# Down projections with the weight sums behind the casts, the last weight buffer taken last, and three attention output tiles ended one after another

## The chip, the cores and the metric

The kernel runs on one core of one Trainium2 chip. The metric is the device time of one execution in microseconds (us). Work is spread over five engines with a queue of their own each, and every queue is worked off in order: TensorE (PE, matrix products), VectorE (DVE), ScalarE (ACT), GpSimd (POOL) and SyncE (SP, which here issues nearly all transfers from HBM). An instruction that must wait holds up all that stands behind it in its queue.

## The reference

A decoder trunk of two layers on one sequence of 512 positions and 1024 channels, in float32. Layer 0 mixes tokens with a gated DeltaNet; then keys and values are projected once; layer 1 uses causal sliding-window attention on them. Each layer ends with a gated feed-forward part (FFN):

```
def conv_gated_mlp(hn, w_up, conv_w, conv_b, w_down):
    u = causal_dwconv(hn @ w_up, conv_w, conv_b)
    gate, val = jnp.split(u, 2, axis=-1)
    return (jax.nn.silu(gate) * val) @ w_down
```

with w_up from 1024 to 2 x 2816 channels and w_down from 2816 back to 1024. The change concerns `@ w_down` of both layers and the end of the attention's output projection `@ w_o`.

## The kernel before

Every large product is made of three matmuls in a reduced format: a weight block in a stage buffer is split by `cast` into a high part `whi` (a copy on ACT, line 132) and a low part `wlo` (a subtraction on DVE, line 133); activations are split likewise, and PE adds high x high, high x low, low x high. `cast_to` (lines 155 and 156) does the same into a part of a weight buffer that `weights()` has taken. There are three buffers each for `whi` and `wlo`, two stages named `stage`, and a third one, `st` in the profile, which every third load of a down projection uses. A cast must wait until PE has read the buffer that it reuses; a load must wait until the last cast has read its stage. SP issues the loads in the order of the program.

The FFN is done in two groups of columns of the inner dimension per layer (12 and 10 tiles of 128), so there are four down projections. Each works through four column pairs of the output (256 columns, `m2` 0 to 3), and for each of them `seven_products` does a Strassen-Winograd scheme: instead of eight products of half-size blocks seven, with sums of weight blocks made on DVE. The weights of a column pair come in two loads, block u = 0 and u = 1 (three and three, or three and two, pairs of k tiles), and a stage holds four kinds of 128-column pieces A11, A12, A21, A22. Per block the code

- adds A22 to A21 (line 1063), casts the first half of the stage, and makes two products ("B11" and "B21", banks `d` and `g` of PSUM),
- makes A11 = A21 - A11 and A12 = A12 - A11 (lines 1071, 1072), casts the second half, and makes two products ("T1" and "T4", banks `s` and `p`, or `d` again for odd column pairs),
- makes A22 = A22 - A11 (line 1080).

After the products of block 1 the results are added to h (`add`, line 1057). I call these two rounds the second phase when block 1 is meant. In the third phase both blocks' first halves are cast again, for the products "T2" and "B22", and A22 is cast with `cast_to` into `w4`, for the product "T3" (bank `g` or `p`). The generators of column pairs 0 and 1 are advanced in turns (0, 1, 0, 0, 1, 1), pairs 2 and 3 run alone; the last pair of the last group is done plainly. The order within each queue is set by a scheduler from the code's order and from estimated times, so the lines of several generators mix.

The stage of block 0 becomes free with its piece of `w4` (line 156), and SP then loads a block of a later column pair, or of the next up projection (line 122), into it.

In the attention, the output projection of the first three of eight tiles is drawn into the stream of the scores; the last k tile of these three is added at the end (line 1380) when the last heads' values are there, and line 1382 adds the tiles to h. `ah` and `al` are the high and the low part of the attention's values. The other five tiles are cast and multiplied afterwards (`out_tile`, `mm3`).

Of the kernel before, what the change touches and what calls it, by code (L numbers as in the profile page):

```python
# [12 lines left out]
ALU = mybir.AluOpType  # L13
# [4 lines left out]
P = 128  # L18
# [23 lines left out]
def kernel(  # L42
# [27 lines left out]
    V, S, G, PE, SP = nc.vector, nc.scalar, nc.gpsimd, nc.tensor, nc.sync  # L70
# [9 lines left out]
    def nm(s):  # L80
        cnt[0] += 1
        return f"{s}_{cnt[0]}"
# [30 lines left out]
    def bank(tag):  # L113
        return psum.tile([P, T], F32, tag=tag, bufs=BANKS[tag], name=nm(tag))

    def const(shape, dt=F32, s="c"):
        return cp.tile(list(shape), dt, name=nm(s))


    def load_stage(w, r0, kt, c0):  # L120
        st = wpool.tile([P, 8, 256], F32, tag="stage", bufs=2, name=nm("stage"))
        SP.dma_start(st[:, :kt, :], tiles_of(w, r0, kt, c0))
        return st
# [4 lines left out]
    def cast(st, kt, half, m=P):  # L128
        hi = wpool.tile([P, 8, P], F32R, tag="whi", bufs=3, name=nm("whi"))
        lo = wpool.tile([P, 8, P], F32R, tag="wlo", bufs=3, name=nm("wlo"))  # L130
        src = st[:, :kt, half * P : half * P + m]
        S.copy(hi[:, :kt, :m], src)  # L132
        V.tensor_tensor(lo[:, :kt, :m], src, hi[:, :kt, :m].bitcast(F32), op=ALU.subtract)  # L133
        return hi, lo
# [14 lines left out]
    def weights():  # L149
        return [wpool.tile([P, 8, P], F32R, tag=t, bufs=3, name=nm(t)) for t in ("whi", "wlo")]  # L150

    def cast_to(w, at, src):
        n = src.shape[1]
        hi, lo = [t[:, at : at + n, :] for t in w]
        S.copy(hi, src)
        V.tensor_tensor(lo, src, hi.bitcast(F32), op=ALU.subtract)
# [50 lines left out]
    first = wpool.tile([P, 8, 256], F32, tag="stage", bufs=2, name=nm("stage"))  # L207
# [55 lines left out]
    for k in range(KD):  # L263
        ps = bank("g") if k % 2 else bank("s")
# [136 lines left out]
    nk = const([P, 8, NC], s="nk")  # L401
# [365 lines left out]
    for i, line in enumerate(ORDER):  # L767
        for word in line.split():
            a, n = word[0], [int(d) for d in word[1:]]
# [41 lines left out]
    def wide(role):  # L811
        return pair(nxt("wide", YROLE), F32R)
# [6 lines left out]
    for h2 in range(HV // 2):  # L819
        a, b = wide("G"), wide("L")  # L820
# [11 lines left out]
    hT = [h4[:, m, :] for m in range(4)] + [h22[m // 2][:, m % 2, :] for m in range(4)]  # L832
# [14 lines left out]
    for m2 in range(KD // 2):  # L847
        sts = [load_stage(a_w_out[0], 1024 * u, 8, 256 * m2) for u in range(2)]
        for j in range(2):
            m = 2 * m2 + j  # L850
            ps = bank("d")
            for u in range(2):
                w = cast(sts[u], 8, j)
# [185 lines left out]
    def seven_products(sts, srcs, parts, sevens, hp, odd):  # L1039
        h11, h12, h21, h22 = [hp[:, i, HALF[u]] for i in range(2) for u in range(2)]  # L1040
        n = len(sevens)

        def blocks(u):
            e, o = slice(0, 2 * len(parts[u]), 2), slice(1, 2 * len(parts[u]), 2)
            return sts[u][:, e, 0:P], sts[u][:, o, 0:P], sts[u][:, e, P : 2 * P], sts[u][:, o, P : 2 * P]

        def product(ps, w, at, form, u, first=True, step=2):
            for i, k in enumerate(parts[u]):
                hi, lo = sevens[k][form]
                wk = at + step * i  # L1050
                kw = dict(skip_group_check=not first)
                PE.matmul(ps, w[0][:, wk, :], hi, start=first and k == 0, stop=False, **kw)  # L1052
                PE.matmul(ps, w[0][:, wk, :], lo, start=False, stop=False, **kw)  # L1053
                PE.matmul(ps, w[1][:, wk, :], hi, start=False, stop=k == n - 1, **kw)  # L1054

        def add(dst, ps):
            V.tensor_tensor(dst, dst, ps, op=ALU.add)

        a, b, d, c = [bank(t)[:, 0:256] for t in ("d", "g", "s", "d" if odd else "p")]
        for u in range(2):  # L1060
            A11, A12, A21, A22 = blocks(u)
            nk, end = len(parts[u]), u == 1
            V.tensor_tensor(A21, A21, A22, op=ALU.add)
            w = cast(sts[u], 2 * nk, 0)
            product(a, w, 0, "B11", u)
            if end:
                add(h11, a)
            product(b, w, 1, "B21", u)
            if end:
                add(h11, b)  # L1070
            V.tensor_tensor(A11, A21, A11, op=ALU.subtract)
            V.tensor_tensor(A12, A12, A11, op=ALU.subtract)
            w = cast(sts[u], 2 * nk, 1)
            product(d, w, 0, "T1", u)
            if end:
                add(h22, d)
            product(c, w, 1, "T4", u)
            if end:
                add(h21, c)
            V.tensor_tensor(A22, A22, A11, op=ALU.subtract)  # L1080
            yield
        e = bank("p" if odd else "g")[:, 0:256]
        w4 = weights()
        for u in range(2):
            w = cast(sts[u], 2 * len(parts[u]), 0)
            product(a, w, 0, "T2", u, first=False)
            product(d, w, 1, "B22", u, first=False)
            cast_to(w4, 4 * u, blocks(u)[3])

        add(hp.rearrange("p u (v t) -> p (u v) t", v=2)[:, 1:4, :], a.unsqueeze(1).to_broadcast([P, 3, 256]))  # L1090
        add(h12, d)
        for u in range(2):
            product(e, w4, 4 * u, "T3", u, step=1)
        add(hp[:, 1, :].rearrange("p (u t) -> p u t", u=2), e.unsqueeze(1).to_broadcast([P, 2, 256]))
        yield
# [68 lines left out]
    def attention(h):  # L1164
# [6 lines left out]
        for kv in range(2):  # L1171
# [3 lines left out]
            for i in range(2):  # L1175
                ps = bank("d")
# [115 lines left out]
        def values(u):  # L1292
            p, n0 = u // 2, 2 * (u % 2)
            g = p // 2
            if n0 == 0:
                heads[p] = bank("p")
            po = heads[p]
            for i in range(2):
                pT, kb0, W = heads[u, i]
                nt = W // P  # L1300
                for kb in range(nt):
                    for j in range(2):
                        PE.matmul(  # L1303
                            po[half[j], (n0 + i) * P : (n0 + i + 1) * P],
                            Vp[:, kb0 + kb, 64 * g : 64 * g + 64],
                            pT[:, (j * nt + kb) * P : (j * nt + kb + 1) * P],
                            start=kb == 0,
                            stop=kb == nt - 1,
                        )
            if n0 == 0:  # L1310
                return
            if p % 2 == 0:
                at[:] = [wide("G"), wide("L")]
            a, b = at[0][:, p % 2, :], at[1][:, p % 2, :]
            split(po[:], a, b)
            ah.append(a)
            al.append(b)


        def out_tile(m, sts={}):  # L1320
            if m % 2 == 0:
                sts[m // 2] = load_stage(b_w_o[0], 0, 8, 128 * m)
            return bank("d"), cast(sts[m // 2], 8, m % 2)
# [10 lines left out]
        def late_outputs(opened, ks):  # L1334
            for k in ks:
                for ps, w in opened:
                    yield from one_by_one(ps[:], w, k, ah[k], al[k], False, False)

        at, opened = [], []

        def dense():
            for p in range(2, 8):
                yield from query(p)
            yield from early_outputs(opened)

        def take(stream, n):
            for _ in range(n):
                next(stream, None)
# [8 lines left out]
        with tc.manual_schedule(engines={mybir.EngineType.PE}):  # L1357
            stream = dense()
            for u in range(16):
                scores(u)  # L1360
                if u > 1:
                    values(u - 2)
                if u == 1:
                    take(stream, 8)
                if u > 0:
                    turn_back(u - 1)
                take(stream, 4 if u == 1 else 12 if u < 12 else 11)
            for _ in stream:
                pass
            rest = late_outputs(opened, range(begun, KD - 1))  # L1370
            take(rest, 9)
            turn_back(15)
            values(14)
            take(rest, 5)
            values(15)
            for _ in rest:
                pass
            for i in range(3):
                for m, (ps, w) in enumerate(opened):
                    PE.matmul(ps[:], w[i % 2][:, KD - 1, :], (ah, ah, al)[i][-1], start=False, stop=i == 2)  # L1380
                    if i == 2:
                        V.tensor_tensor(hT[m], hT[m], ps[:], op=ALU.add)
        for m in range(3, KD):
            ps, w = out_tile(m)
            mm3(ps[:], w, KD, ah, al)
# [59 lines left out]
```

## Time and profile before

| what | value |
|---|---|
| runs before | 1421.04, 1417.68, 1419.02 us; median 1419.02 |
| profiled execution | 1418.66 us, its span 1416.8 us |
| granted PE clock over the span | 0.998 |
| busy PE, DVE, ACT, POOL | 98%, 78%, 53%, 1% |
| the four down projections with their neighbourhood | 657 to 722, 828 to 886, 1178 to 1242, 1347 to 1392 us |
| end of the three drawn tiles of the attention | 1015 to 1021 us |

A timeline row gives the start in us, the duration, the engine, the line, the operation, out<-in by the names in the program, the shape, and how many like rows it stands for; in brackets the idle time of the engine ahead of it and what released it. A row of waits gives who waited for whom, and then the total, how often, and the longest. The rows on transfers give the KB of each and the median time from issue to landing.

### The profile page before, as it was taken

How to read it: one execution, taken by the hardware profiler on the slowest of the kernel's cores; microseconds unless marked ns; L12 is line 12 of the kernel's file. 1: busy time of each engine (PE TensorE's matmuls, PEld its weight loads, DVE VectorE, ACT ScalarE, POOL GpSimd, SP SyncE). 2: the span in 40 equal slices, each digit the busy share in tenths (PEclk: the TensorE clock that was granted, in tenths of full speed). 3: DMA queues.
4: the chain of work that ended last, by engine and by line, in shares of the span. 5: the costliest groups of instructions: out<-in, count | busy, mean ns of one | idle time of the engine just before them, and what ended most of it. 6: DMA issues, size and time to landing. Idle time of an engine off the chain costs nothing.

```text
span 1416.8 us, 21740 instructions
## 1 busy us (share of the span) xinstructions
PE 1384.8 (98%) x8362; PEld 1166.5 (82%) x8362; DVE 1109.1 (78%) x2072; ACT 748.0 (53%) x1470; POOL 15.7 (1%) x37
## 2 busy tenths in 40 slices
PE   7999999999999999999999999999999999999997
PEld 5787888878877888888988889778788888988897
DVE  4996886968856447879878889788658888878996
ACT  7764576656647325444335446567544444444543
POOL 1000000000100000000000000000000000000000
PEclk9999999999999999999999999999999999999999
DMA  5333254172465323221443223322132221432222
GB/s 160 90 104 115 80 174 124 60 230 84 143 221 157 119 86 115 90 90 46 134 149 119 75 73 108 109 76 76 60 112 86 93 90 59 137 107 86 95 75 75
DMA packets 162299, 151.80 MB, mean 107 GB/s; under 512 B 24148, under 2 KB 150677, under 8 KB 162197
## 3 DMA queue, kind: packets, MB, share of 16 engines
q1 hardware_dynamic: 159938, 150.22, 33.0%
q8 instruction: 66, 1.08, 0.3%
q10 hardware_dynamic: 2259, 0.20, 0.1%
q14 instruction: 36, 0.29, 0.1%
HBM read 133.60 MB, written 15.75 MB: 105 GB/s over the span
## 4 chain that ended last, share of the span: by engine, by line
PE 85%; DVE 7%; DMA 4%; ACT 2%; issue 1%; SPq 0%; DVEq 0%; ACTq 0%
PE d L162 20%; PE d L164 20%; PE d L163 20%; PE g L198 2%; DVE wlo L133 2%; PE d L1207 1%; PE d L1211 1%; PE d L1209 1%; PE d L1054 1%; PE d L1052 1%; PE d L1053 1%; PE s L1054 1%; PE p L1303 1%; PE s L659 1%; PE s L1052 1%
## 5 line engine op out<-in xcount | busy, mean ns | idle before, releaser
L162 PE MATMUL d<-xh,whi 128*128 128x512 f32 x1128 | 444.2, 394 | 0.2
L163 PE MATMUL d<-xl,whi 128*128 128x512 f32 x1128 | 444.0, 394 | 0.0
L164 PE MATMUL d<-xh,wlo 128*128 128x512 f32 x1128 | 442.1, 393 | 0.8 <-DVE wlo L133 0.5
L132 ACT CAST whi<-stage 128x1024 fp32r<-128x1024 f32 (+2 forms) x234 | 227.4, 976 | 249.7 <-PE d L163 170.3
L133 DVE TENSOR_TENSOR wlo<-stage,whi 128x1024 fp32r<-128x1024 f32 (+2 forms) x234 | 263.3, 1128 | 70.2 <-ACT whi L132 69.3
L164 PEld LDWEIGHTS d<-xh,wlo 128*128 128x128 f32 x1128 | 211.6, 188 | 45.5 <-DVE wlo L133 1.0
L162 PEld LDWEIGHTS d<-xh,whi 128*128 128x128 f32 x1128 | 211.7, 188 | 44.8 <-ACT xh L172 0.5
L163 PEld LDWEIGHTS d<-xl,whi 128*128 128x128 f32 x1128 | 211.7, 188 | 43.1 <-issue 0.5
L280 DVE SCALAR_TENSOR_TENSOR acc<-d,cwc,acc 128x511 f32<-128x511 f32 (+2 forms) x96 | 70.6, 738 | 8.7 <-ACT acc L277 7.8
L913 DVE TENSOR_TENSOR sz<-d,p6s 128x512 f32<-128x512 f32 x59 | 40.6, 688 | 43.4 <-PE d L164 41.2
L935 ACT ACTIVATE dt<-dt 128x512 f32<-128x512 f32 x44 | 27.8, 632 | 78.3 <-DVE dt L918 78.3
L918 DVE SCALAR_TENSOR_TENSOR dt<-sz,fcw,dt 128x511 f32<-128x511 f32 (+1 forms) x60 | 44.8, 747 | 1.8 <-ACT dt L916 0.9
L918 DVE SCALAR_TENSOR_TENSOR va<-sz,fcw,va 128x511 f32<-128x511 f32 (+1 forms) x58 | 43.3, 747 | 0.9
L561 DVE TENSOR_TENSOR sT<-sT,p6s 64x31 f32<-64x31 f32 (+15 forms) x124 | 40.9, 330 | 2.0
L555 DVE TENSOR_TENSOR p6s<-sN,sT 64x31 f32<-64x31 f32 (+15 forms) x124 | 40.7, 328 | 1.9
L1276 ACT ACTIVATE dt<-dt,sm 128x256 f32<-128x256 f32 (+1 forms) x64 | 30.1, 471 | 21.5 <-DVE sm L1259 21.5
L132 ACT CAST whi<-st 128x768 fp32r<-128x768 f32 (+1 forms) x30 | 23.7, 791 | 30.1 <-PE p L1053 5.8
L913 DVE TENSOR_TENSOR zl<-d,p6s 128x512 f32<-128x512 f32 x29 | 20.0, 688 | 17.8 <-PE d L164 17.8
L682 ACT ACTIVATE rq<-o 128x128 f32<-128x128 f32 x64 | 19.0, 301 | 25.0 <-DVE o L677 22.0
L937 DVE TENSOR_TENSOR va<-dt,va 128x512 f32<-128x512 f32 x44 | 30.4, 690 | 1.2
L133 DVE TENSOR_TENSOR wlo<-st,whi 128x768 fp32r<-128x768 f32 (+1 forms) x30 | 26.8, 899 | 2.2 <-ACT whi L132 2.2
L916 ACT ACTIVATE dt<-sz,normc,fcw 128x512 f32<-128x512 f32 x30 | 24.4, 815 | 6.5 <-DVE sz L913 6.2
(769 smaller groups left out, 2873.2 us busy)
## 6 DMA issues: line engine op xcount, KB each, us to landing
stage<-in_ffn_w_up_dram SPq DMA_DIRECT2D x44, 1024.0 KB, 4.7
stage<-in_a_w_in_dram SPq DMA_DIRECT2D x23, 1024.0 KB, 5.5
stage<-in_ffn_w_down_dram SPq DMA_DIRECT2D x16, 768.0 KB, 4.3
stage<-in_a_w_out_dram SPq DMA_DIRECT2D x8, 1024.0 KB, 5.1
st<-in_ffn_w_down_dram SPq DMA_DIRECT2D x8, 768.0 KB, 5.2
zd<-sz SPq DMA_DIRECT2D x16, 256.0 KB, 2.6
od<-o SPq DMA_DIRECT2D x16, 256.0 KB
stage<-in_b_w_q_dram SPq DMA_DIRECT2D x4, 1024.0 KB, 5.0
```

The source lines that it names most:

```text
L132: S.copy(hi[:, :kt, :m], src)
L133: V.tensor_tensor(lo[:, :kt, :m], src, hi[:, :kt, :m].bitcast(F32), op=ALU.subtract)
L162: PE.matmul(ps, hi[:, k, :m], xh[k], start=first and k == 0, stop=False)
L163: PE.matmul(ps, hi[:, k, :m], xl[k][:], start=False, stop=False)
L164: done.append(PE.matmul(ps, lo[:, k, :m], xh[k], start=False, stop=last and k == kt - 1))
L280: V.scalar_tensor_tensor(acc[:, d:], ps[:, : T - d], col, acc[:, d:], op0=ALU.mult, op1=ALU.add)
L555: V.tensor_tensor(tv, N[:, s, s + 1 : 32].unsqueeze(2).to_broadcast([64, n, m]), Tm[:, s : s + 1, 0:m].to_broadcast([64, n, m]), op=ALU.mult,)
L561: V.tensor_tensor(Tm[:, s + 1 : 32, 0:m], Tm[:, s + 1 : 32, 0:m], tv, op=ALU.subtract)
L913: V.tensor_tensor(u[:], ps[:], rs[:], op=ALU.mult)
L918: V.scalar_tensor_tensor(acc[:, d:], u[:, : T - d], tap(2 - d, t), acc[:, d:], op0=ALU.mult, op1=ALU.add)
L937: V.tensor_tensor(b[:], a[:], b[:], op=ALU.mult)
L1276: S.activation(ej, ej, AF.Exp, bias=ngm[:, i : i + 1], scale=-1.0, accum_out=den[:, i : i + 1])
```

## The change

Three things are edited.

- The sums of the weights are put into a function `sums(u)`: A11 as before, and then A12 and A22 less A11 in one joint operation on both (all 256 columns of the odd k pieces). For block 0 it stands behind the product "T4", for block 1 behind the third phase's cast of block 0.
- `w4` is taken after both casts of the third phase, and its two `cast_to` follow both pairs of products.
- At the end of the attention, the loops over the three tiles and over the three matmuls of a tile are swapped, so each tile gets its high, low and high matmul and its addition to h, one tile after another.

```
+        def sums(u):
+            A11, _, A21, _ = blocks(u)
+            nk = len(parts[u])
+            V.tensor_tensor(A11, A21, A11, op=ALU.subtract)
+            odds = sts[u][:, 1 : 2 * nk : 2, :].rearrange("p k (v c) -> p k v c", v=2)
+            V.tensor_tensor(odds, odds, A11.unsqueeze(2).to_broadcast([P, nk, 2, P]), op=ALU.subtract)
+
         for u in range(2):
...
             if end:
                 add(h11, b)
-            V.tensor_tensor(A11, A21, A11, op=ALU.subtract)
-            V.tensor_tensor(A12, A12, A11, op=ALU.subtract)
             w = cast(sts[u], 2 * nk, 1)
             product(d, w, 0, "T1", u)
...
             if end:
                 add(h21, c)
-            V.tensor_tensor(A22, A22, A11, op=ALU.subtract)
+            else:
+                sums(u)
             yield
         e = bank("p" if odd else "g")[:, 0:256]
+        for u in range(2):
+            w = cast(sts[u], 2 * len(parts[u]), 0)
+            if u == 0:
+                sums(1)
+            product(a, w, 0, "T2", u, first=False)
+            product(d, w, 1, "B22", u, first=False)
         w4 = weights()
         for u in range(2):
-            w = cast(sts[u], 2 * len(parts[u]), 0)
-            product(a, w, 0, "T2", u, first=False)
-            product(d, w, 1, "B22", u, first=False)
             cast_to(w4, 4 * u, blocks(u)[3])
...
-            for i in range(3):
-                for m, (ps, w) in enumerate(opened):
+            for m, (ps, w) in enumerate(opened):
+                for i in range(3):
                     PE.matmul(ps[:], w[i % 2][:, KD - 1, :], (ah, ah, al)[i][-1], start=False, stop=i == 2)
-                    if i == 2:
-                        V.tensor_tensor(hT[m], hT[m], ps[:], op=ALU.add)
+                V.tensor_tensor(hT[m], hT[m], ps[:], op=ALU.add)
```

In the kernel after, lines 1057 and below 200 are the same; 1063 becomes 1071, the sums are lines 1064 and 1066, 1380 becomes 1390. PE, ACT, POOL and SP issue as many rows as before, DVE thirty fewer.

DVE's queue in the first column pair of the first down projection, from the low half of block 1's second cast on, before (`stage_993` holds block 0 and `stage_994` block 1, `h4` is the part of h for the pair; `wlo_1021`, `wlo_1023` and `wlo_1019` are the third phase's two casts and `w4`):

```order
L133 TENSOR_TENSOR wlo_1016_6319<-stage_994_6181,whi_1015_6318 128x768
L1071 TENSOR_TENSOR stage_994_6181<-stage_994_6181 128x3x128
L1057 TENSOR_TENSOR h4_4550<-h4_4550,d_997_6187 128x256
L1072 TENSOR_TENSOR stage_994_6181<-stage_994_6181 128x3x128
L1057 TENSOR_TENSOR h4_4550<-h4_4550,g_998_6188 128x256
L1080 TENSOR_TENSOR stage_994_6181<-stage_994_6181 128x3x128
L1057 TENSOR_TENSOR h4_4550<-h4_4550,s_999_6189 128x256
L133 TENSOR_TENSOR wlo_1021_6347<-stage_993_6179,whi_1020_6346 128x768
L1057 TENSOR_TENSOR h4_4550<-h4_4550,p_1000_6190 128x256
L156 TENSOR_TENSOR wlo_1019_6345<-stage_993_6179,whi_1018_6344 128x384
L133 TENSOR_TENSOR wlo_1023_6371<-stage_994_6181,whi_1022_6370 128x768
L156 TENSOR_TENSOR wlo_1019_6345<-stage_994_6181,whi_1018_6344 128x384
```

and after (`wlo_1019` and `wlo_1021` are now the third phase's casts, `wlo_1023` is `w4`):

```order
L133 TENSOR_TENSOR wlo_1016_6315<-stage_994_6181,whi_1015_6314 128x768
L1057 TENSOR_TENSOR h4_4550<-h4_4550,d_997_6187 128x256
L133 TENSOR_TENSOR wlo_1019_6340<-stage_993_6179,whi_1018_6339 128x768
L1057 TENSOR_TENSOR h4_4550<-h4_4550,g_998_6188 128x256
L1057 TENSOR_TENSOR h4_4550<-h4_4550,s_999_6189 128x256
L1064 TENSOR_TENSOR stage_994_6181<-stage_994_6181 128x3x128
L1057 TENSOR_TENSOR h4_4550<-h4_4550,p_1000_6190 128x256
L1066 TENSOR_TENSOR stage_994_6181<-stage_994_6181 128x3x256
L133 TENSOR_TENSOR wlo_1021_6364<-stage_994_6181,whi_1020_6363 128x768
L156 TENSOR_TENSOR wlo_1023_6386<-stage_993_6179,whi_1022_6385 128x384
L156 TENSOR_TENSOR wlo_1023_6386<-stage_994_6181,whi_1022_6385 128x384
```

Block 1's sums now stand behind the adds to h, the last of them behind the add of bank `p`, and the first L156 stands behind the cast of block 1, which reads what the joint sum wrote.

ACT's queue at the same place before, the third phase's casts and `w4`'s:

```order
L132 CAST whi_1020_6346<-stage_993_6179 128x768
L155 CAST whi_1018_6344<-stage_993_6179 128x384
L155 CAST whi_1018_6344<-stage_994_6181 128x384
L132 CAST whi_1022_6370<-stage_994_6181 128x768
L132 CAST whi_1024_6416<-stage_996_6185 128x768
```

and after:

```order
L132 CAST whi_1018_6339<-stage_993_6179 128x768
L132 CAST whi_1020_6363<-stage_994_6181 128x768
L155 CAST whi_1022_6385<-stage_993_6179 128x384
L155 CAST whi_1022_6385<-stage_994_6181 128x384
L132 CAST whi_1024_6413<-stage_996_6185 128x768
```

Both parts of `w4` moved behind the cast of block 1.

PE's queue at the end of the attention before (`at_9827` is the high part, `at_9828` the low one; `d_9627`, `d_9702` and `d_9778` are the three tiles):

```order
L1380 MATMUL d_9627<-at_9827,whi_9628 128x512
L1380 MATMUL d_9702<-at_9827,whi_9703 128x512
L1380 MATMUL d_9778<-at_9827,whi_9779 128x512
L1380 MATMUL d_9627<-at_9827,wlo_9629 128x512
L1380 MATMUL d_9702<-at_9827,wlo_9704 128x512
L1380 MATMUL d_9778<-at_9827,wlo_9780 128x512
L1380 MATMUL d_9627<-at_9828,whi_9628 128x512
L1380 MATMUL d_9702<-at_9828,whi_9703 128x512
L1380 MATMUL d_9778<-at_9828,whi_9779 128x512
```

and after:

```order
L1390 MATMUL d_9611<-at_9811,whi_9612 128x512
L1390 MATMUL d_9611<-at_9811,wlo_9613 128x512
L1390 MATMUL d_9611<-at_9812,whi_9612 128x512
L1390 MATMUL d_9686<-at_9811,whi_9687 128x512
L1390 MATMUL d_9686<-at_9811,wlo_9688 128x512
L1390 MATMUL d_9686<-at_9812,whi_9687 128x512
L1390 MATMUL d_9762<-at_9811,whi_9763 128x512
L1390 MATMUL d_9762<-at_9811,wlo_9764 128x512
L1390 MATMUL d_9762<-at_9812,whi_9763 128x512
```

The first tile's last read of its weight buffers moved from the seventh place to the third, and the first use of the low part `at_9812` with it.

More of the change, by code (lines that the diff above doesn't have):

```diff
@@ L1059, in seven_products @@
         a, b, d, c = [bank(t)[:, 0:256] for t in ("d", "g", "s", "d" if odd else "p")]
+        def sums(u):
[4 more added lines that the diff above has]
+            V.tensor_tensor(odds, odds, A11.unsqueeze(2).to_broadcast([P, nk, 2, P]), op=ALU.subtract)
         for u in range(2):
-            A11, A12, A21, A22 = blocks(u)
+            _, _, A21, A22 = blocks(u)
             nk, end = len(parts[u]), u == 1
```

## The prediction

> **What bounds the kernel now.** I read the page's totals first, then TensorE's (PE) waits in each of the four down projections, then the timeline of every engine there, and last the end of the attention.
>
> ```profile
> PE 1384.8 (98%) x8362; PEld 1166.5 (82%) x8362; DVE 1109.1 (78%) x2072; ACT 748.0 (53%) x1470; POOL 15.7 (1%) x37
> ```
>
> PE is busy for 98%; the change removes no matmul, so it can move only PE's idle time. The waits of PE (total us, times, longest) in the first down projection (657 to 722 us):
>
> ```profile
> PE d L1052 <- ACT whi L132: 0.5, 1, 0.5
> PE s L1054 <- DVE wlo L133: 0.4, 1, 0.4
> PE d L1054 <- DVE wlo L133: 0.4, 1, 0.4
> ```
>
> and in the second (828 to 886 us):
>
> ```profile
> PE d L1054 <- DVE wlo L133: 1.0, 1, 1.0
> PE s L1054 <- DVE wlo L133: 0.3, 1, 0.3
> PE d L1052 <- ACT whi L132: 0.2, 1, 0.2
> ```
>
> Two kinds stand there: waits for a low half that VectorE (DVE) has not yet cast, which the change aims at, and one wait for a high half (ACT). The timeline says what the latter is. PE and SP in the first interleaved pair of columns:
>
> ```profile
> 668.43 0.39 PE L1054 MATMUL d<-at,wlo 128*128 128x256 f32 x1 [0.39 <-DVE wlo L133]
> 671.76 0.28 PE L1054 MATMUL p<-m,wlo 128*128 128x256 f32 x1
> 678.37 0.28 PE L1054 MATMUL g<-m,wlo 128*128 128x256 f32 x1
> 679.11 0.39 PE L1052 MATMUL d<-at,whi 128*128 128x256 f32 x1 [0.46 <-ACT whi L132]
> 691.20 0.28 PE L1052 MATMUL d<-qT,whi 128*128 128x256 f32 x1
> 673.42 1.74 SPq L1034 DMA_DIRECT2D stage<-in_ffn_w_down_dram  x2
> ```
>
> DVE and ACT there:
>
> ```profile
> 672.51 0.41 DVE L1057 TENSOR_TENSOR h<-h,p 128x256 f32<-128x256 f32 x1
> 672.84 0.55 DVE L156 TENSOR_TENSOR wlo<-stage,whi 128x384 fp32r<-128x384 f32 x1
> 673.31 0.95 DVE L133 TENSOR_TENSOR wlo<-stage,whi 128x768 fp32r<-128x768 f32 x1
> 674.18 0.55 DVE L156 TENSOR_TENSOR wlo<-stage,whi 128x384 fp32r<-128x384 f32 x1
> 671.43 0.52 ACT L155 CAST whi<-stage 128x384 fp32r<-128x384 f32 x1 [0.59 <-DVE stage L1080]
> 672.02 0.84 ACT L132 CAST whi<-stage 128x768 fp32r<-128x768 f32 x1
> 678.23 1.57 ACT L132 CAST whi<-stage 128x768 fp32r<-128x768 f32 x2 [5.38 <-DMA stage<-in_ffn_w_down_dram]
> ```
>
> The L156 of 672.84 is the last reader of the first block's stage. It ends at 673.39; SP issues the next load into that stage at 673.42 (a second one 1.37 us later, behind the L156 of 674.18), ACT starts its cast at 678.23, and PE, out of work since 678.4, starts at 679.11. So a loop of buffer release, load and cast already has no slack: whatever delays that L156 delays PE.
>
> **The sums (lines 1071, 1072, 1080 become 1064 and 1066).** Three 128x384 operations of 0.55 each (the form of L156) become one of 0.55 and a joint one of 128x768, for which I take the 0.95 of the 128x768 row: 1.50 for 1.65, fifteen columns, two blocks, at most 4.5 us of DVE work, none of it on PE's path by itself. Placed behind the second cast, they no longer stand ahead of the low half: the first 0.4 wait goes almost wholly (the joint operation on the block before costs 0.4 of head start, and the last sum saves more). I take -0.4 for it, bounds 0 and -0.5, and the last product of the second phase, 671.76 now, ends at 671.65 instead of 672.04. But in the order after, the adds to h stand ahead of the second block's joint sum, and the cast of the third phase needs that sum.
>
> **The late weights (w4).** Now their first L156 comes behind both third-phase casts. Its end, step by step from the p product's end: 671.65, add to h 0.41, joint sum 0.95, ACT cast 0.84, low half 0.95, L156 0.55, less about 0.1 for overlap of neighbours on DVE: 675.25, against 673.39. First load +1.85; the second L156 follows at once, 675.7 against 674.73. From issue to cast it took 4.8 (673.42 to 678.23), so the cast starts at 680.05 and PE at 680.95: +1.85, its idle 2.5 instead of 0.7. Bounds for the load: the page's median and 0.6 more than the 4.8, as both loads now start half a microsecond apart:
>
> ```profile
> stage<-in_ffn_w_down_dram SPq DMA_DIRECT2D x16, 768.0 KB, 4.3
> ```
>
> I stay near 4.8, because that load already had a neighbour. The Trainium skill (DMA: Bandwidth & Descriptors, "Anatomy of one DMA") gives a load issued from GpSimd 2.0 us plus its bytes at 436 GB/s, as an estimate 3.8 us for this one and 5.6 for the two sharing the engines; by the first PE would start 0.9 us sooner than I take, by the second 0.8 later. This case's loads, from SP, took 4.3 and more, so the measured row decides.
>
> Behind that restart the low-half wait of 0.4 goes, and with it its own slow start and those of two products that now come singly drawn forward, 0.1 each (a first matmul after a wait takes 0.39 for 0.28): -0.75. The next pair's start, 691.20 now, comes at 692.25: **+1.1** for the pair, bounds +0.6 and +1.7. Columns three and four show no wait of PE before; their casts run ahead, and I cost them nothing. That cover ends in one place, where the group hands over to the next up projection:
>
> ```profile
> 713.50 0.55 DVE L156 TENSOR_TENSOR wlo<-stage,whi 128x384 fp32r<-128x384 f32 x1
> 715.16 0.42 DVE L1057 TENSOR_TENSOR pz<-pz,d 128x256 f32<-128x256 f32 x1 [0.19 <-PE d L1054]
> 714.08 3.23 SPq L122 DMA_DIRECT2D stage<-in_ffn_w_up_dram  x2
> 720.30 1.05 ACT L132 CAST whi<-stage 128x1024 fp32r<-128x1024 f32 x1 [4.38 <-DMA stage<-in_ffn_w_up_dram]
> 721.44 0.47 PE L162 MATMUL d<-xh,whi 128*128 128x512 f32 x1
> stage<-in_ffn_w_up_dram SPq DMA_DIRECT2D x44, 1024.0 KB, 4.7
> ```
>
> The load of 714.08 lands only just in time for 721.44. After, the L156 that frees its stage comes behind the add of 715.16, and 1.1 later with the pair: 716.25 + 0.42 + 0.55, so the load is issued at 717.2, +3.1. It took 6.1 before with a second load 2.9 behind it, and 4.7 in the median; at 5.5 it lands at 722.7, the cast takes 1.05, PE starts at 723.9 instead of 721.44: **+2.5** for this down projection (bounds +1.7 and +3.6), of which 1.1 was counted above.
>
> **The other three** have the same loop:
>
> ```profile
> 842.92 0.28 PE L1054 MATMUL p<-S,wlo 128*128 128x256 f32 x1
> 845.36 0.37 SPq L1034 DMA_DIRECT2D st<-in_ffn_w_down_dram  x1
> 849.37 0.62 ACT L132 CAST whi<-st 128x512 fp32r<-128x512 f32 x1 [4.94 <-DMA st<-in_ffn_w_down_dram]
> 850.05 0.38 PE L1052 MATMUL d<-at,whi 128*128 128x256 f32 x1 [0.20 <-ACT whi L132]
> 1198.35 2.30 ACT L132 CAST whi<-stage 128x768 fp32r<-128x768 f32 x3 [5.00 <-DMA stage<-in_ffn_w_down_dram]
> 1364.51 1.31 SPq L1034 DMA_DIRECT2D stage<-in_ffn_w_down_dram  x2
> 1368.06 0.62 ACT L132 CAST whi<-stage 128x512 fp32r<-128x512 f32 x1 [4.47 <-DMA stage<-in_ffn_w_down_dram]
> ```
>
> In the second and fourth the second block is smaller (two pieces of k instead of three). The p product, which ended at 843.20, ends at about 843.0; behind it come an add to h 0.41, a sum of 0.42 (the width of such an add) and the joint one of 0.69 (the form of the 128x512 rows), the cast 0.62, the low half 0.69 and L156 0.55, less 0.3 of overlaps: 846.1 to 846.4, against an issue at 845.36. PE restarts 1.1 later than 850.05, and the 1.0 saved ahead only makes the wait there longer. The 0.3 saved later is taken by a new wait for the cast behind the joint sum. So **+1.3** where norm work shares ACT and DVE, and **+1.0** in the fourth. The third is the first pair over again, **+1.2**, without the hand-over, since its next up load goes into a stage freed one column earlier.
>
> **The end of the attention.**
>
> ```profile
> 1016.44 0.84 PE L1380 MATMUL d<-at,whi 128*128 128x512 f32 x3
> 1016.87 2.95 ACT L132 CAST whi<-stage 128x1024 fp32r<-128x1024 f32 x3 [2.14 <-PE d L1380]
> 1017.97 0.50 PE L162 MATMUL d<-sy,whi 128*128 128x512 f32 x1 [0.68 <-ACT whi L132]
> 1018.91 0.50 PE L162 MATMUL d<-sy,whi 128*128 128x512 f32 x1 [0.22 <-ACT whi L132]
> 1019.87 0.50 PE L162 MATMUL d<-sy,whi 128*128 128x512 f32 x1 [0.22 <-ACT whi L132]
> 1014.75 0.69 DVE L169 TENSOR_TENSOR at<-p,at 128x512 fp32r<-128x512 f32 x1 [6.44 <-ACT at L168]
> ```
>
> ACT's three casts wait for the three weight buffers, all read until the last three of nine matmuls. After, the first tile's last read is the third matmul, four places (0.92 us) before 1016.44; the low half of the attention that it needs is there at 1015.44, just in time for 1015.52. The first cast then starts at 1015.95 and ends when the ninth matmul starts its successor: the 0.68 wait and its slow restart go, the second stays at about 0.4, the third goes, since the third tile is no longer drawn forward. **-1.4**, bounds -0.8 and -1.95 (all three with restarts).
>
> **Sum:** 2.5 + 1.3 + 1.2 + 1.0 - 1.4 = +4.6 on the profiled execution's 1418.66 (span 1416.8 and 1.86 around it; 0.36 under the median of 1419.02): 1423.3. A measurement here can tell about 0.2%, 2.8 us, from no change.
>
> **Rivals.** *Faster:* the buffer loop does not bind, because w4's first cast still runs where it ran. The trace shows that this is possible: at 671.43 ACT cast w4 a microsecond before the last add to h. It decides whether the load is issued by 674, where the savings ahead of it still pay for its delay. Then only the low-half waits fall: the 0.4 and 0.4 of the first, twice (for the third), 1.0 and 0.3, twice: -4.2, and -1.4: 1413.1. Against it stand the in-order queues: DVE has no row in which the first L156 could pass the joint sum. *Same:* each load lands in 4.3 rather than 4.8 and the hand-over stays hidden: the four terms become 0.6, 0.9, 0.7 and 0.6, less 1.4: +1.4, 1420.1. Against it: the up load's 6.1. *That allotting in order of use changes nothing* is half true: the cast of the third phase came ahead of w4's on ACT before as well; it is the later casts that count, and they are in the sum.
>
> **Chances.** Slower as worked out 0.70; about the same 0.18; faster 0.12. The upper bounds together (3.6 + 1.6 + 1.6 + 1.2 - 0.8 is 7.2) give 1425.9, and with the 0.36 to the median 1426.3: the range ends at 1426.5. Downwards it goes through most of the second case, to 1418.0.
>
> **What would show it.** Right: SP's load of 673.42 at about 675.2, PE's wait behind 678.4 at 2.2 us or more and put down to ACT's cast, an up start with a wait near 723 to 724, no wait for low halves at 668 and 844, first cast of the output tiles near 1016.0. Wrong: the load still issued by 674, or PE drawn so far ahead that the p product ends a microsecond earlier.

## The result, and the profile after

The changed kernel takes 1426.51 us in the median of its runs (1425.82 to 1429.5), the kernel before 1418.35 in the same session: a ratio of 1.0062, 95% interval 1.0037 to 1.0087, or +8.2 us. The forecast was 1423.3. The side was right and the size too small: the forecast had +4.6, and the median lies just past the upper end of its range, 1426.5. Medians in this document leave out three executions far above the rest (1524 us of the kernel before, 3058 of e3, 1533 of e6).

The page's totals of the changed kernel; no matmul has gone or come, and PE is busy 3.5 us longer than before:

```profile
PE 1388.3 (97%) x8362; PEld 1170.7 (82%) x8362; DVE 1109.2 (78%) x2042; ACT 745.3 (52%) x1470; POOL 15.7 (1%) x37
```

PE's waits in the four down projections (657 to 730 us with the hand-over, 828 to 886, 1178 to 1242, 1347 to 1392):

```profile
PE d L1052 <- ACT whi L132: 2.4, 2, 2.3
PE d L162 <- ACT whi L132: 2.2, 1, 2.2
...
PE d L1052 <- ACT whi L132: 3.1, 3, 2.0
PE d L1054 <- DVE wlo L133: 0.2, 1, 0.2
...
PE d L1052 <- ACT whi L132: 2.5, 2, 2.3
...
PE d L1052 <- ACT whi L132: 2.8, 2, 2.3
```

The waits for low halves (`wlo`) in the second phases are gone, and in their place stands one wait of 2.0 to 2.3 us per down projection for a high half, where there had been 0.46 in the first. The timeline shows the chain that the prediction named. DVE, ACT, SP and PE in the first pair of columns:

```profile
670.86 0.42 DVE L1057 TENSOR_TENSOR h<-h,p 128x256 f32<-128x256 f32 x1
671.20 0.95 DVE L1066 TENSOR_TENSOR stage<-stage 128x768 f32<-128x768 f32 x1
672.26 0.83 ACT L132 CAST whi<-stage 128x768 fp32r<-128x768 f32 x1 [5.15 <-DVE stage L1066]
673.13 0.96 DVE L133 TENSOR_TENSOR wlo<-stage,whi 128x768 fp32r<-128x768 f32 x1 [0.97 <-ACT whi L132]
674.00 1.02 DVE L156 TENSOR_TENSOR wlo<-stage,whi 128x384 fp32r<-128x384 f32 x2
674.58 0.96 SPq L1034 DMA_DIRECT2D stage<-in_ffn_w_down_dram  x2
679.38 1.57 ACT L132 CAST whi<-stage 128x768 fp32r<-128x768 f32 x2 [5.46 <-DMA stage<-in_ffn_w_down_dram]
680.26 0.39 PE L1052 MATMUL d<-at,whi 128*128 128x256 f32 x1 [2.27 <-ACT whi L132]
```

Add to h, joint sum, cast, low half, L156, load, cast, PE: each waits for the one ahead of it. This execution is 0.79 us ahead of before's when it comes to this place, so the load is 1.95 late (674.58 + 0.79 - 673.42).

To see where the time went I matched the two profiles matmul by matmul and took how far the changed kernel falls behind in each stretch. The last column is a second profile of the same kernel (below, e10):

| stretch | forecast | after | after, again |
|---|---|---|---|
| start to 640 us (untouched code) | 0 | -0.79 | -0.19 |
| first down projection, column pair | +1.1 | +1.01 | +1.06 |
| its hand-over to the up projection | +1.4 | +3.47 | +1.21 |
| second down projection, pair | +1.3 | +1.17 | +2.61 |
| second, its end, and key and value projections | 0 | -1.27 | -1.23 |
| end of the attention | -1.4 | -1.24 | -1.25 |
| third down projection, pair | +1.2 | +2.91 | +2.99 |
| fourth, pair | +1.0 | +2.99 | +3.33 |
| all others | 0 | -0.14 | -0.17 |
| sum | +4.6 | +8.11 | +8.36 |

Three terms (the first pair, the second, the attention) are good to 0.2 in the first profile; the hand-over, the third and the fourth are 1.7 to 2.1 too small. Those three have something in common. Windows of the changed kernel (us, then busy PE, PEld, DVE, ACT and POOL with their counts, the granted clock of PE, the DMA share and GB/s), two for each of four waits, the one with the wait and the one behind it:

```profile
676.40:679.80 3.40, 1.59 (x14) 1.39 (x12) 1.54 (x3) 0.42 (x1) 0.00 (x0) 1.00 0.96 324
679.80:683.20 3.40, 2.94 (x22) 2.74 (x23) 3.02 (x6) 1.88 (x3) 0.00 (x0) 1.00 0.25 89
720.70:724.20 3.50, 1.28 (x11) 1.08 (x10) 0.87 (x2) 1.04 (x1) 0.00 (x0) 0.99 0.94 296
724.20:727.60 3.40, 3.28 (x8) 2.11 (x9) 1.57 (x2) 1.60 (x2) 0.00 (x0) 0.51 0.73 257
...
1202.00:1205.40 3.40, 1.59 (x11) 1.39 (x12) 2.41 (x4) 2.30 (x3) 0.00 (x0) 1.00 0.66 233
1205.40:1208.80 3.40, 3.40 (x19) 3.40 (x18) 2.30 (x5) 0.00 (x0) 0.00 (x0) 0.50 0.00 0
1208.80:1212.20 3.40, 3.40 (x30) 3.40 (x30) 2.90 (x5) 1.66 (x3) 0.00 (x0) 0.99 0.00 0
1372.70:1376.10 3.40, 1.10 (x9) 0.90 (x8) 2.99 (x7) 2.51 (x5) 0.00 (x0) 1.00 0.96 328
1376.10:1379.50 3.40, 3.40 (x18) 3.40 (x17) 2.20 (x4) 0.63 (x1) 0.00 (x0) 0.50 0.02 9
```

Behind the waits of 724, 1205 and 1376 PE runs at half its clock for 3.4 us: it starts 18 or 19 matmuls of the down projection (behind 1205 and 1376), where a full window (1208.80) has 30. Behind that of 680, which is just as long, it does not. So the same wait costs its length, or its length and some 1.5 us more. What decides that is the subject of the later experiments.

### The profile page after: what moved, and what is told of

Read it like the earlier page. It is cut to its first block, busy times and chain, and to the rows that moved or that the text cites. A ratio compares the mean times of both kernels' runs of the same rounds, so it can differ in the third digit from the quotient of the medians.

```text
span 1424.9 us, 21700 instructions
## 1 busy us (share of the span) xinstructions
PE 1388.3 (97%) x8362; PEld 1170.7 (82%) x8362; DVE 1109.2 (78%) x2042; ACT 745.3 (52%) x1470; POOL 15.7 (1%) x37
## 4 chain that ended last, share of the span: by engine, by line
PE 88%; DVE 5%; DMA 3%; ACT 2%; issue 1%; SPq 0%; DVEq 0%; ACTq 0%
PE d L162 20%; PE d L164 20%; PE d L163 20%; PE g L198 2%; PE d L1052 1%; PE d L1217 1%; PE d L1054 1%; PE d L1221 1%; PE d L1219 1%; PE d L1053 1%; DVE wlo L133 1%; PE s L1052 1%; PE s L1054 1%; PE s L1053 1%; PE s L659 1%; DMA stage<-in_ffn_w_down_dram 1%
```

## The experiments

My theory: the loop of buffer release (third phase's cast of block 1, `w4`, load, next cast) binds, and with it the hand-over. The rivals: the delay comes from the sums in their new place; or the loop doesn't bind and something else (contention of the loads, the order of the column pairs) does it. The later question: what the idle time costs beyond its length. All runs were timed against the kernel before on the same chip.

**e1, the attention's end alone.** Before, with the two loops swapped.

```
-            for i in range(3):
-                for m, (ps, w) in enumerate(opened):
+            for m, (ps, w) in enumerate(opened):
+                for i in range(3):
```

> Before, with only the end of the attention changed (three output tiles ended singly). The theory, that this part is worth what the trace of after shows there (its matmuls gain 1.24 us between 1005 and 1036 us), expects -1.2 us, about 0.1% faster, within what a measurement can tell. The rival, that the gain at this place is given back later by the stage loads, expects 0.0.

Measured 1417.16 against 1417.4, ratio 1.0001 (0.999 to 1.0013). The stretch itself gives -1.25 in e1's profile, just as in the changed kernel's, but the time doesn't resolve it: stretches that no edit touched differ by -0.89 to +1.26 between e1's execution and before's. That is also the yardstick for the table above: pairs repeat to 0.3, the hand-over to 0.9 (both kernels are the same there).

**e2, the sums alone.** Before, with `sums(u)` in the changed kernel's places; `w4` as before.

```
-            V.tensor_tensor(A11, A21, A11, op=ALU.subtract)
-            V.tensor_tensor(A12, A12, A11, op=ALU.subtract)
...
-            V.tensor_tensor(A22, A22, A11, op=ALU.subtract)
+            else:
+                sums(u)
...
             w = cast(sts[u], 2 * len(parts[u]), 0)
+            if u == 0:
+                sums(1)
```

> Before, with only the weight sums moved and joined; w4 is taken and cast where it was. Theory (the loss comes from the late release of block 0's stage by w4's cast, not from the sums): the first load of the first pair is issued near 673.4 as before, the waits for low halves of 0.4 to 1.0 us go, the second block's restart stays near 679; -0.75, -0.5, -0.75 and -0.5 for the four pairs, in all -2.5 us, 1416. Rival (the joint sum behind the adds to h delays all that follows): the same idle of 2.4 us as after, and +5 us or more.

1413.79 against 1417.4, 0.9974 (0.9963 to 0.9986): faster. SP's loads in the first down projection, then PE's waits there:

```profile
674.66 2.30 SPq L1034 DMA_DIRECT2D stage<-in_ffn_w_down_dram  x2
```

```profile
PE d L1052 <- ACT whi L132: 0.6, 1, 0.6
```

e2 is 1.22 us behind at this place, so the load stands where it stood (673.44 for 673.42), and the waits for low halves are gone: the four pairs give -1.22, -1.33, -0.98 and -1.43. That is more than the -2.5 that I expected. The sums in their new place are not the cause.

**e3, the late `w4` alone.** Before, with `w4` taken after both casts of the third phase.

```
-        w4 = weights()
         for u in range(2):
...
+        w4 = weights()
+        for u in range(2):
             cast_to(w4, 4 * u, blocks(u)[3])
```

> Before, with only w4 taken and cast behind both third-phase casts; the sums stay where they were. Theory: block 0's stage is released 1.3 us later (674.7 for 673.4), so +1.3 in each of the four pairs, and about +2.5 at the hand-over to the up projection, +7 to +8 in all, and up to 3 more where the longer idle lowers the granted clock. Rival (late w4 is harmless without the late sums): 0 to +1.

1423.52 against 1417.4, 1.0043 (1.0026 to 1.006): slower, by 6.1 us for the 7 to 8 expected. The load at 674.75 is 0.86 late after the 0.47 that e3 is behind, and the pairs cost +0.29, +2.18, +0.59 and +1.22 (in the second PE still waits for low halves too, 2.0 us in all; before 1.3). Alone the late `w4` delays the load by less than half of the changed kernel's 1.95; in e3 the cast of block 1 does not wait for a joint sum behind the adds to h. The parts don't add up: -0.2, -3.6 and +6.1 make +2.3 for the measured +8.

**e4, the changed kernel with `w4` early again.**

```
-        w4 = weights()
-        for u in range(2):
+            if u == 0:
+                w4 = weights()
             cast_to(w4, 4 * u, blocks(u)[3])
```

> After, with w4 taken behind block 0's third-phase cast and its first half cast there, ahead of block 1's cast (sums and attention as in after). Theory: the sum of the two other parts, -2.5 and -1.2, so -3.7 us against before, about 1414.7, and no idle of over 1 us at the second block's restart. Rival (the sums cost): slower than before by 3 us or more.

1413.62 against 1417.4, 0.9972 (0.996 to 0.9984). The whole loss goes, and the gain of the sums comes back. The same two views:

```profile
672.47 2.31 SPq L1034 DMA_DIRECT2D stage<-in_ffn_w_down_dram  x2
```

```profile
PE d L1052 <- ACT whi L132: 0.5, 1, 0.5
```

The load stands at before's place (672.47 + 0.97 is 673.44). e2, e3 and e4 together show the loop: the late `w4` is what makes the change slow.

**e5, `w4` late in column pairs 0 and 1 only,** early in 2 and 3 (`early` is true for these). It separates the restart in the first pair from the hand-over, which belongs to the last columns.

```
+            if early:
+                if u == 0:
+                    w4 = weights()
+                cast_to(w4, 4 * u, blocks(u)[3])
+        if not early:
+            w4 = weights()
+            for u in range(2):
+                cast_to(w4, 4 * u, blocks(u)[3])
```

> After, with w4 early (behind block 0's cast) in column pairs 2 and 3 of every down projection, and late as in after in pairs 0 and 1. Theory: the wait of 2.4 us at the hand-over from the first down projection to the up projection comes from w4 being late in pair 3 alone, so it goes (the hand-over's +3.5 becomes about -0.9, as with early w4 everywhere), while the restarts of the second blocks still wait 2.2 to 2.5 us: +4.7 us against before instead of +8. Rival (the up projection starts late because the whole group is late): the hand-over keeps +2 or more, +7 to +8 in all.

1423.61 against 1418.71, 1.003 (1.0017 to 1.0043). The hand-over's cost goes (-0.04; -0.9 was expected), since its first load is issued on time again, with the second well behind it (both within 3.25 us, before within 3.23):

```profile
716.86 3.25 SPq L122 DMA_DIRECT2D stage<-in_ffn_w_up_dram  x2
723.07 1.05 ACT L132 CAST whi<-stage 128x1024 fp32r<-128x1024 f32 x1 [4.35 <-DMA stage<-in_ffn_w_up_dram]
```

(e5 is 2.8 us behind before's 714.08 and 720.30 here.) The four pairs still cost +2.21, +1.15, +2.96 and +3.30. This time the first pair is among the dear ones, and its clock shows why:

```profile
678.00:681.40 3.40, 1.35 (x12) 1.15 (x10) 1.36 (x3) 0.52 (x1) 0.00 (x0) 1.00 1.01 344
681.40:684.80 3.40, 3.04 (x14) 3.04 (x15) 2.69 (x3) 1.78 (x3) 0.00 (x0) 0.51 0.18 63
```

**e6, the turns of the column pairs shifted by one** in the changed kernel (`turns = [1]` for `[0]`), so that other pairs use the third stage.

> After, with the counter that gives every third load the third stage begun one later, so that at the end of the first down projection the next up load finds a stage freed one column pair earlier, as it does at the end of the third. Nothing else is changed. Theory: the hand-over of the first down projection loses its wait (-3.5 to -4.4 us), and that of the second, which now has the tight rotation, gives less than 1.5 back, as the key and value projection has slack: +4 to +6 against before. Rival (stage rotation does not matter): +8.

1423.01 against 1418.71, 1.0034 (1.0021 to 1.0047). The hand-over comes out at -0.89, as in e1, e2 and e4, whose up load was on time; the pairs still cost +1.09, +2.59, +2.97 and +3.06. The hand-over depends on which stage the last columns use; the restarts don't.

**e7, the long wait filled.** In the changed kernel, 18 matmuls whose result is not used stand behind the third phase of column pair 0, so that PE is busy in the wait but no less late with its own work.

```
+            for i in range(18):
+                mm = PE.matmul(z, hi[:, 0:P], hi, start=True, stop=True)
+                behind(mm, last)
+                last = mm
```

> After, with 18 matmuls of 128x256 without use (into a bank that nobody reads) behind the first column pair's last product in each down projection, where PE waits 2.2 to 2.5 us for the second block of the other pair. They take about 18 x 0.12 = 2.2 us and fit into the wait. Theory (the clock is lowered because of the idle time): PE restarts when it did, but the granted clock behind it, 0.51 and 0.52 in the third and fourth down projection of after, is 1.0, and each of the two gains 1.5 us: -3 against after, +5 against before. Rival (the lowered clock has another cause, such as the load that lands or the burst of casts): the clock stays at 0.5 there and the time at +8 or above.

1423.05 against 1418.71, 1.003 (1.002 to 1.0041). In e7 no window between 306 and 1418 us is at half clock. Where the clock changes it does so at the edges of windows of 3.41 us (see below), and such edges lie here at 851.55, 854.96, 1203.12 and 1206.53. From PE's last own product to its restart pass 2.05 us in the second pair and 2.34 in the third; of these 2.05 and 2.13 lie in one window. These two windows, each with the one behind it:

```profile
851.50:855.00 3.50, 3.50 (x30) 3.40 (x30) 2.84 (x6) 2.79 (x5) 0.00 (x0) 1.00 0.99 335
855.00:858.40 3.40, 3.40 (x30) 3.40 (x30) 3.40 (x8) 1.48 (x3) 0.00 (x0) 1.00 0.12 41
1203.10:1206.50 3.40, 3.21 (x25) 2.81 (x24) 2.36 (x4) 2.13 (x3) 0.00 (x0) 1.00 0.72 252
1206.50:1209.90 3.40, 3.40 (x30) 3.40 (x30) 3.39 (x7) 0.17 (x1) 0.00 (x0) 1.00 0.02 5
```

The pairs now cost +1.19, +1.16, +1.56 and +1.15, the hand-over +1.41: within 0.4 of the terms that I forecast. The third and fourth fall by 1.35 and 1.84 against the changed kernel, though 18 matmuls more are done. So that part of the loss is the half clock and not the late work. The third wait shows it best; the first and the fourth are cut by an edge in e7 (at most 1.3 and 1.5 us of them lie in one window) and might have kept the clock without the filling.

**e8, the best order so far:** e4, with the add behind "T4" moved behind `w4`'s first part, so that block 1's sums stand ahead of it on DVE.

```
-            if end:
-                add(h21, c)
-            else:
+            if not end:
                 sums(u)
...
             cast_to(w4, 4 * u, blocks(u)[3])
+            if u == 0:
+                add(h21, c)
```

> The kernel of e4 (after with w4 early), with the add to h of bank p moved behind w4's first half cast, so that block 0's stage is released before the p product ends (about 671.2 instead of 673.4 in the first pair). Theory (release decides the restart): the last waits of 0.4 to 0.7 us at the restarts go, -1.5 to -1.8 us against e4, of which the key and value projection gives back up to 0.4; about -5.3 us against before. Rival (the restart is limited by something else, the load or the cast): as e4, -4.

1412.89 against 1418.71, 0.995 (0.9932 to 0.9968). The pairs give -2.38, -1.88, -2.00 and -2.12, and PE has no wait left in the first. But +2.30 is lost at the key and value projections, as in e2 and e4 (+2.2 and +2.0). A part of that is the clock again: each of the three has one window at half clock behind that wait (at 887, 884 and 887 us for e2, e4 and e8). PE's wait there, and DVE at 883 us:

```profile
PE d L164 <- DVE wlo L156: 1.8, 1, 1.8
```

```profile
883.20 2.73 DVE L173 SCALAR_TENSOR_TENSOR xl<-pz,normc,xh 128x512 fp32r<-128x512 f32 x4
885.85 1.09 DVE L156 TENSOR_TENSOR wlo<-f,whi 128x256 fp32r<-128x256 f32 x3
```

PE arrives earlier, DVE doesn't: the low half of the key weights stands behind four rows of the norm.

**e9, e8 with the key weights' first cast ahead of that norm.**

```
+        kw = [cast_rows(key_weights, 0)]
         kxh, kxl = normed(h, NKV)
...
+                mm3(ps[:], cast(st, 8, i) if kv else kw[0] if i == 0 else cast_rows(key_weights, 1), KD, kxh, kxl)
```

> Changed kernel with w4's first part early, the add behind the second phase's third product moved behind that part's cast, and one more edit: the first cast of the key weights for the key and value projections now stands ahead of the norm that precedes them. In the three profiles with the early w4 (the sums alone, the early w4, the early w4 with the deferred add) PE waits 1.7 to 1.85 us at 883 to 886 us for a low half that stands behind the norm's L173 rows on DVE, and gives back 2.0 to 2.3 us of what the second down projection had gained; two of them show a granted clock of 0.57 and 0.64 behind that wait. Theory (the gain is lost there only because DVE's queue is in that order): the wait goes, the stretch 866 to 900 comes out near before's instead of 2.3 above it, 1410 to 1411 against 1412.9. Rival (PE is there bound by the norm itself, whichever row stands first): the L173 come later, PE waits as long for the normed activations, 1412.5 to 1413.5. Slower rival: the early cast holds a weight buffer that the down projection's last pair needs, so a new wait of 1 us or more stands between 860 and 880: 1414.

1408.8 against 1418.61, 0.9935 (0.992 to 0.995). The wait for L156 is gone, and where e8 has lost 2.7 us by 893 us, e9 has gained 1.3; a new wait, for `va`, which DVE still has to make, stands at 899 us, so from 866 to 1000 us e9 is level with before, where e8 lost 2.35:

```profile
PE d L162 <- DVE va L1195: 1.9, 1, 1.9
```

e9 beats both kernels: 9.8 us under before, some 17 under the changed one. Beside the 2.4 us won here, e9's profile has no half clock between 50 us and its last three, where e8's has it at 299, 429 and 886 us.

**e10, the changed kernel once more,** for a second profile.

> The changed kernel itself, once more, for a second profile and more runs. The four long waits of PE in the first column pairs are fixed by the program, so they must stand again: 2.0 to 2.5 us each, put down to ACT's cast. If the granted clock behind a wait is a matter of the moment (theory), the stretches at about half clock may stand behind others of these waits than the third and fourth, and each such stretch costs 1.3 to 1.8 us on top of its wait; with two to three of them the time is 1425 to 1427. Rival (the dip belongs to the third and fourth waits by what stands around them): dips at 1206 and 1376 again and at no other pair's first wait. Either way the hand-over to the up projection costs 1.4 to 3.5 us.

1426.25 against 1418.61, 1.0055 (1.0037 to 1.0073). Third and fourth wait have the half clock again, the hand-over not, and now the second pair has it. Windows of the second pair, first of the changed kernel's earlier profile, then of this one:

```profile
850.40:853.90 3.50, 2.35 (x20) 2.14 (x18) 2.81 (x5) 1.63 (x3) 0.00 (x0) 1.00 0.66 228
853.90:857.30 3.40, 2.51 (x20) 2.51 (x21) 3.40 (x7) 2.63 (x5) 0.00 (x0) 1.00 0.44 154
```

```profile
850.50:853.90 3.40, 1.36 (x11) 1.15 (x10) 2.85 (x6) 3.26 (x6) 0.00 (x0) 1.00 1.06 364
853.90:857.30 3.40, 3.40 (x17) 3.40 (x17) 2.10 (x4) 1.00 (x2) 0.00 (x0) 0.50 0.01 3
```

The instructions are the same and the wait as long (the longest is 2.0 us in both). In the first it is cut in two by the edge at 853.9, about 1.1 and 0.9 us on either side; in the second it lies wholly ahead of it. The pair costs +1.17 and +2.61: the half clock is worth 1.4 us. The ten runs of e10 agree: the three with the highest granted clock over the span (0.997) took 1420.6 to 1422.9 us, the three with the lowest (0.991) 1429.2 to 1431.7.

## Why the prediction was off

**Right: the mechanism and its place.** The in-order queues held: the first L156 did not pass the joint sum; the load is 1.95 late for the 1.85 forecast; it was there 4.8 us after issue (679.38 - 674.58), as taken; the wait of 2.27 is ACT's cast, and PE restarts 1.94 late; the pair costs +1.01 for +1.1, +1.06 again. The two estimates drawn from the Trainium skill (DMA: Bandwidth & Descriptors, "Anatomy of one DMA"), 3.8 and 5.6 us, lie on either side of that load. e4 takes the late `w4` away and the loss is gone. The waits for low halves at 668 and 844 are gone. The rival on the faster side needed a load issued by 674: e4 is that case, and takes 3.8 us less than before for the rival's 5.6.

**Right: the attention.** -1.24 and -1.25 for -1.4. ACT's cast starts after the first tile's third matmul, at 1016.04 if the 3.45 us that this execution is behind there are taken off, forecast 1015.95; of three waits one short one is left:

```profile
1018.97 0.71 PE L1390 MATMUL d<-at,whi 128*128 128x512 f32 x2
1019.49 2.94 ACT L132 CAST whi<-stage 128x1024 fp32r<-128x1024 f32 x3 [1.31 <-PE d L1390]
1020.68 0.41 PE L162 MATMUL d<-sy,whi 128*128 128x512 f32 x1
1021.54 0.50 PE L162 MATMUL d<-sy,whi 128*128 128x512 f32 x1 [0.21 <-ACT whi L132]
```

**The step that failed: "its idle 2.5 instead of 0.7", taken as the whole price.** The sum has the terms +1.2 for the third and +1.0 for the fourth down projection, "the first pair over again"; they measured +2.91 and +2.99 (+2.99 and +3.33 again). The idle was about as forecast, 2.3 us; the rest is the half clock behind it, which no term had. Before could not show it: its granted clock is 1.00 from 16 to 1412 us, and the most that PE idles there in one of the windows told of next is 1.7 us. The upper bounds of the sum (1.6, 1.6, 1.2) left this out too. That the first pair agrees with its term in both profiles, and the second in one, is owed to where the clock's windows lay: in e5 the first pair cost +2.21.

**When it strikes.** In all twelve profiles the granted clock changes on a grid of 3.41 us whose position differs from execution to execution, and a stretch at half clock lasts one such window. I aligned windows with that grid in each profile and added up PE's idle time in each, against the clock of the next window (from 17 to 1400 us; a matmul whose record is missing counts as idle):

| PE idle in a window, us | windows | followed by half clock |
|---|---|---|
| under 1.3 | 4801 | 0 |
| 1.3 to 1.5 | 14 | 1 |
| 1.5 to 1.85 | 21 | 12 |
| over 1.85 | 14 | 14 |

About half of the window decides. A wait of 2.3 us has 1.7 of itself in one window in (3.41 - 2.3 + 2 x 0.6) / 3.41 = 0.68 of the positions, so at 1.5 us it costs about 1.0 on average beyond its length. Four such waits (0.9 for the second, of 2.0 us) make +3.9, and my 4.6 would have been 8.5; less the 1.25 of the next point, 7.25, against the +8.2 and +7.6 of the two sessions. This estimate comes after the fact, from this case's own counts. e7, where the waits are filled, has the time without the half clock: +4.3 against before, for my +4.6. The Trainium skill (TensorE: Matmul & The Clock Gate, Part 1) has a free-running window of 3413 ns, which the grid here agrees with, and lets the clock fall after one idle window or more; here a window idle for about half sufficed, and the measurement decides.

**The hand-over: right in e7 and e10, too small in the first profile.** The first up load was issued 3.2 late (716.45 + 0.79 - 714.08, forecast 3.1), but it took 6.4 us instead of the 5.5 taken (landed at 722.85), and the half clock followed:

```profile
716.45 1.68 SPq L122 DMA_DIRECT2D stage<-in_ffn_w_up_dram  x2
722.94 1.04 ACT L132 CAST whi<-stage 128x1024 fp32r<-128x1024 f32 x1 [6.70 <-DMA stage<-in_ffn_w_up_dram]
724.04 0.72 PE L162 MATMUL d<-xh,whi 128*128 128x512 f32 x1 [2.22 <-ACT whi L132]
```

In e10 and e7, with the same two loads half a microsecond apart, it took 5.2 and 5.4, and the hand-over cost +1.21 and +1.41 for the +1.4 of the sum. Why the load takes 6.4 in one execution I have not settled. The close neighbour alone is not it: with the second load 2.8 to 2.9 behind, the first took 6.1 in before and e5, and 5.0 to 5.3 in e1, e2, e4, e8 and e9. The hand-over goes with it: -0.04 in e5, -0.8 to -0.9 in the other five.

**Not foreseen: 1.25 us given back behind the second down projection.** PE came to the key and value projections later and found there none of the short waits of before (0.29, 0.26, 0.45 and 0.30 behind their usual start intervals, 1.3 in all). What was a cover for a delay was a loss for a gain: e2, e4 and e8 came early and lost 2.0 to 2.3 at the same place, the half clock there included. That the total came out so near the end of the range is partly luck: without these 1.25 us it would have been +9.4.

## What to carry to other kernels

In in-order queues a buffer's last reader is the start of the next load: before moving it, follow release, load, cast and first use round the loop, and if the loop has no slack, every instruction put ahead of that reader is paid in full. Price a wait of PE by its length, and add some 1.5 us, times the chance that it falls into one window, where it is longer than about half of the clock's window of 3.41 us. A part that wins by itself (the sums, -3.6 us) and one that loses by itself (the late `w4`, +6.1) can meet on the same chain and cost more than their sum (+8), so time them apart before judging the whole.

## What the runs showed of the hardware

- PE's granted clock falls to half for one window of 3.41 us after a window in which PE idled for more than 1.85 us (14 of 14), and never under 1.3 us (0 of 4801). Each cost 1.2 to 1.8 us where PE had work (the first pair in e5 against the changed kernel, the third and fourth against e7). The grid's position differs between executions, so the same program pays at different waits: at 45, 724, 1205 and 1376 us in one profile of the changed kernel, at 45, 301, 854, 1205 and 1376 in the other.
- That can also be a part of the scatter of untouched code. The stretch up to 640 us lies between -2.91 us (e6) and +2.97 (e8) against before; e8 has two windows at half clock there (299 and 429 us), e6 none. It is not the whole: before has none either, and lies 2.91 above e6.
- Two 1 MB loads issued 0.47 us apart from SP took 5.0 to 6.4 us for the first and 7.2 to 9.0 for the second (e3, e7, e10 and the changed kernel); 2.8 to 2.9 apart, they took 5.0 to 6.1 and 5.7 to 6.4 (before, e1, e2, e4, e5, e8, e9). The second pays for a close neighbour; that the first does is not shown.
